# One order of wide and narrow products in the up projection, and twelve pairs of places for the weight parts of the first projections

## The chip, the core and the metric

The kernel runs on one core of one Trainium2 chip. The metric is the device time of one execution in microseconds. The time before is 1240.1 us, the median of three runs (1239.98 to 1240.11).

## What is computed

One layer of a hybrid decoder trunk, in float32, for 256 tokens of width 2048 with 16 learned tokens ahead of them (272 rows in all). Cut to what matters:

```python
h = concatenate([meta, x])                        # 272 x 2048
u = rms_norm(h, g_pre_mix)
z_pool, v_conv, g_conv, gate_a, gate_b = split(u @ w_in)   # 1024, 1024, 1024, 2048, 2048 columns
y_a = causal_multiscale_pool(z_pool, w_pool_grp, pool_scale) @ w_pool_out
y_b = conformer_conv(v_conv, g_conv, ...) @ w_conv_out
m = sigmoid(gate_a) * y_a + sigmoid(gate_b) * y_b
h = h + rms_norm(m @ w_o, g_post_mix)
u = rms_norm(h, g_pre_mlp)
f = square(relu(u @ w_up)) @ w_down               # 2048 -> 8192 -> 2048
h = h + rms_norm(f, g_post_mlp)
return h[16:]
```

## The kernel before

**Every product in three.** Each float32 operand is split into two parts in TensorE's reduced float32 format: the high part is a rounding copy by ScalarE, the low part the rest, a subtraction by VectorE. A product of two operands is then three matmuls: high by high, high by low, and low by high.

**The stream of weights.** All weights come as chunks of 128 x 2048 numbers (1 MB) in one fixed list, `stream` (lines 111 to 134). `open_chunk` (L161) takes the next chunk of the list, issues its DMA on SP's queue (L177) and makes two tiles for its parts; the cast (L180) writes the high part `hi`, the subtraction (L183) the low part `lo`. `fetch` (L200) keeps two chunks ahead. The parts live in three rooms each, `lo0` to `lo2` and `hi0` to `hi2`, which chunk n uses as n modulo 3, so a room is written again when the products of the chunk three places back have read it. Two chunks (`spare`, L128) get tiles of their own.

**Places.** A line is 16 numbers, 64 bytes, and four lines are 256 bytes. I call the position of an address within 256 bytes, counted in lines, its place: 0 to 3. `ROOMS` (L143) gives for each room the place where it starts and how many lines it has to spare; `part_tile` (L153) shifts the tile within its room so that the part starts at the wanted place. Before, every low part is at place 1; a high part is at place 2 where its chunk is in `standing_chunks` (the z columns of `w_in`, L117, and `w_up`, L130) and at place 1 elsewhere. The normed input `u` of the first projections lies at place 0, and the input `u2` of the up projection (in the tile `m`) at place 1. Rows of these tiles are whole multiples of 256 bytes, so each slice that a matmul reads has the place of its tile.

**First projections.** Three kinds of product come first: v (columns 1024 to 2047 of `w_in`), g (2048 to 3071) and z (0 to 1023), each in four products of 256 columns, in the order v0, g0, v1, g1, v2, g2, v3, g3, z0 to z3. Each product has two chunks of 8 x 128 rows and two accumulators. The weights are what stands in the array; the 272 columns of `u` stream through. For each of 16 blocks of rows and each accumulator `mm3` (L336) issues three matmuls: the high weights by the high `u`, the high weights by the low `u`, and the low weights by the high `u`: 96 a product. The first product, v0, is interleaved with the transposes that make `u`. While these products run, VectorE works off a queue of other items (`pending`), the taps of the causal convolution above all.

**The middle.** Gates, pool and convolution outputs and the mixing product `o` follow; in them and in the down projection the activations stand in the array and 512 columns of weights stream (`block_t`, L594).

**The MLP.** It runs in four passes over 2048 hidden columns each. A pass has four up products (`project` with `mm2`, L366 and L354) and then four down products (`project_t`). An up product has four weight chunks of 4 x 128 rows and four accumulators of 512 columns: the left 256 gather high by high and low by high, the right 256 gather high by low. `mm2_high` (L344) is one wide matmul over both halves of the accumulator (512 columns, the high and the low part of `u2` side by side); `mm2_low` (L349) is one narrow matmul over the left half (256 columns). For each chunk the kernel goes through the four accumulators, and for each through four blocks of rows, a wide and a narrow matmul for each block. In `mm2` the wide one goes first, but for the last of the 16 blocks: there the narrow one goes first and the wide one, which covers the whole accumulator, carries the flag that ends the accumulation. So each accumulator ends with two narrow and then two wide matmuls in a row, the second wide one being that which begins the next accumulator. When an accumulator is complete, `halves` copies the left half with ScalarE and adds the right one with VectorE; the squared relu and the split for the down projection follow.

The first up product of the first pass is written out by hand (lines 896 to 949), because `u2` is still being made: its first three chunks are worked off in halves of the tokens, all wide ones of a chunk and then all its narrow ones (`up_high`, `up_low`); its last chunk goes through `mm2`.

Of the kernel before, what the change touches and what calls it, by code (L numbers as in the profile page):

```python
# [9 lines left out]
F32R = mybir.dt.float32r  # L10
# [4 lines left out]
P = 128  # L15
CK = 4
CW = 512
# [5 lines left out]
def hybrid_block(ctx: ExitStack, tc: tile.TileContext, ins: dict, out: bass.AP):  # L23
# [7 lines left out]
    KD = D // P  # L31
    w_in = ins["w_in"][0]
# [9 lines left out]
    PW = NG * GD  # L42
# [9 lines left out]
    parts = ctx.enter_context(tc.tile_pool(name="parts", bufs=1))  # L52
# [4 lines left out]
    def f32(ap):  # L57
        return ap.bitcast(F32)

    def acc_tile(name):  # L60
        return psA.tile([P, CW], F32, tag="acc", name=name)
# [38 lines left out]
    def columns(w, k0, nk, c0, shape=(CK, CW)):  # L100

        ck, cw = shape
        return [(w[(k0 + kc) * P:(k0 + kc + ck) * P, c0:c0 + cw]
                 .rearrange("(k p) c -> p k c", p=P), shape) for kc in range(0, nk, ck)]
# [4 lines left out]
    HALF = (2 * CK, CW // 2)  # L109
    HALF_CW = CW // 2  # L110
    stream = []
    for h in range(CC // HALF_CW):
        for c0 in (PW, PW + CC):
            stream += columns(w_in, 0, KD, c0 + h * HALF_CW, HALF)
    standing_chunks = set()
    for h in range(PW // HALF_CW):
        standing_chunks.update(range(len(stream), len(stream) + KD // HALF[0]))  # L117
        stream += columns(w_in, 0, KD, h * HALF_CW, HALF)
    for n in range(2 * D // CW):
        stream += columns(w_in, 0, KD, G0 + n * CW)  # L120
    stream.append((w_grp.rearrange("g (k p) c -> p (g k) c", p=P), (NG * GD // P, GD)))
# [7 lines left out]
    for i in range(NP):  # L129
# [3 lines left out]
        for n in range(NB):  # L133
            stream += columns(w_down, i * KD, KD, n * CW)
    FIRST = KD // HALF[0]
# [1 line left out]
    at = {"n": 0}  # L137

    LINE = 16
    ROOMS = {"lo0": (1, 0), "lo1": (1, 0), "lo2": (1, 0), "hi0": (1, 1), "hi1": (2, 3),  # L143
             "hi2": (1, 1)}
    ready = {}

    def part_room(key, name):
        return parts.tile([P, CK * CW + ROOMS[key][1] * LINE], F32R, tag=key, name=name)

    for key in ROOMS:  # L150
        ready[key] = part_room(key, f"{key[:2]}_{key[2]}")

    def part_tile(tag, n, standing=False):  # L153
        key = f"{tag}{n % 3}"
        room = ready.pop(key) if key in ready else part_room(key, f"{tag}_{n}")
        start = ROOMS[key][0]
        to = 2 if standing else 1
        shift = (to - start) % 4 * LINE
        return room[:, shift:shift + CK * CW]

    def open_chunk():  # L161
        n = at["n"]
        at["n"] += 1
        src, (rows, width) = stream[n]
        raw = raws.tile([P, CK * CW], F32, tag="raw", name=f"raw_{n}")
        if n in spare:
            both = big.tile([P, 2, CK * CW], F32R, tag=spare[n], name=f"parts_{n}")
            hi, lo = both[:, 0, :], both[:, 1, :]
        else:
            hi, lo = part_tile("hi", n, n in standing_chunks), part_tile("lo", n)  # L170
        raw, hi, lo = (t.rearrange("p (k c) -> p k c", k=rows) for t in (raw, hi, lo))
        pieces = rows if n < FIRST + 1 else 1
        k = rows // pieces
        loads = 4 if n < FIRST else 1
        for i in range(loads):
            sl = slice(i * rows // loads, (i + 1) * rows // loads)
            nc.sync.dma_start(raw[:, sl, :], src[:, sl, :])  # L177

        def high(sl):
            nc.scalar.copy(hi[:, sl, :], raw[:, sl, :])  # L180

        def low(sl):
            nc.vector.tensor_sub(lo[:, sl, :], raw[:, sl, :], f32(hi[:, sl, :]))  # L183

        def piece(i):
            def f():
                sl = slice(i * k, (i + 1) * k)
                high(sl)
                low(sl)
            return f  # L190
        todo = [piece(i) for i in range(pieces)]
        if n in spare:
            todo = [lambda: high(slice(0, rows)), lambda: low(slice(0, rows))]
        opened.append((hi, lo, todo))
# [5 lines left out]
    def fetch(ahead=2):  # L200

        for c in range(ahead + 1):
            if c == len(opened) and at["n"] < len(stream):
                open_chunk()
            if c < len(opened):
                split_pieces(c)
        flush()
        return opened.pop(0)[:2]
# [51 lines left out]
    for b in range(2, XB):  # L260
        open_chunk()
        load_x(nc.sync, b)
# [81 lines left out]
    def mm2_high(acc, hi, act, k, cs, start, ts=slice(0, T), stop=False):  # L344
        off = act.shape[3] - T
        nc.tensor.matmul(acc.rearrange("p (a t) -> p a t", a=2)[:, :, ts], hi[:, k[0], cs],  # L346
                         act[:, k[1], :, off + ts.start:off + ts.stop], start=start, stop=stop)

    def mm2_low(acc, lo, act, k, cs):  # L349
        off = act.shape[3] - T  # L350
        nc.tensor.matmul(acc[:, :T], lo[:, k[0], cs], act[:, k[1], 0, off:],  # L351
                         start=False, stop=False)

    def mm2(acc, hi, lo, act, k, cs, first, last):  # L354


        if last:
            mm2_low(acc, lo, act, k, cs)
        mm2_high(acc, hi, act, k, cs, first, stop=last)
        if not last:  # L360
            mm2_low(acc, lo, act, k, cs)

    def acc_tiles(name, n=CW // P):
        return [acc_tile(f"acc_{name}_{j}") for j in range(n)]
# [1 line left out]
    def project(act, nk, evac, name, mm=mm2, width=CW, shape=HALF, fill=0.0):  # L366

        ck, cw = shape
        accs = [acc[:, :width] for acc in acc_tiles(name, cw // P)]
        for kc in range(nk // ck):  # L370
            hi, lo = fetch()
            for j, acc in enumerate(accs):
                for k in range(ck):
                    kk = kc * ck + k
                    mm(acc, hi, lo, act, (k, kk), slice(j * P, (j + 1) * P), kk == 0, kk == nk - 1)
                if kc == nk // ck - 1:
                    flush(1)
                    evac(j, acc)
                if fill:
                    drain(fill * P / cw)  # L380
# [52 lines left out]
    def pieces_to(n):  # L433

        while first["split"] < min(n, (FIRST + 1) * HALF[0]):
            c = first["split"] // HALF[0]
            if c == at["n"]:
                open_chunk()
            opened[c][2].pop(0)()
            first["split"] += 1  # L440
# [212 lines left out]
    hi, lo = fetch()  # L653
    for g in range(NG):
        for j in range(GK):
            q = g * GK + j
            acc = acc_tile(f"acc_grp_{q}")[:, :T]
# [242 lines left out]
    def up_high(kc, t):  # L900

        for k in range(CK):
            for j, acc in enumerate(accs):
                kk = kc * CK + k
                mm2_high(acc, ups[kc][0], u2, (k, kk), slice(j * P, (j + 1) * P),
                         t == 0 and kk == 0, slice(t * P, (t + 1) * P))

    def up_low(kc):
        for k in range(CK):
            for j, acc in enumerate(accs):  # L910
                mm2_low(acc, ups[kc][1], u2, (k, kc * CK + k), slice(j * P, (j + 1) * P))
# [28 lines left out]
    hi, lo = fetch()  # L940
# [3 lines left out]
    for j, acc in enumerate(accs):  # L944
        for k in range(CK):
            kk = 3 * CK + k
            mm2(acc, hi, lo, u2, (k, kk), slice(j * P, (j + 1) * P), False, kk == KD - 1)
        flush(1)
        evac_up(0)(j, acc)
# [65 lines left out]
    n = KD // CK - 3  # L1015
    for kc in range(n):
        hi, lo = fetch()
# [54 lines left out]
```

## Time and profile before

| | |
|---|---|
| Median of three runs | 1240.1 us |
| The profiled execution | 1240.15 us |
| Its span, first to last instruction of the program | 1238.2 us |
| Matmuls, and their share of the span in the profile | 6572, 99% |
| VectorE, ScalarE busy | 65%, 44% |
| Moved by DMA | 237.22 MB, mean 192 GB/s |

The profile is of one execution. Its page gives the busy time of each engine; the chain of work that ended last, followed back from the last instruction to what released each step; and groups of instructions by source line (L346 is line 346 of the kernel). A row of a group reads: line, engine, operation, what it writes and reads, count | busy us, mean ns of one | idle time of the engine ahead of them and what ended it. Matmuls are pipelined: each is shown longer than the step from its start to that of the next, so what a matmul costs is read from starts, not from its length.

### The profile page before, as it was taken

How to read it: one execution, taken by the hardware profiler on the slowest of the kernel's cores; microseconds unless marked ns; L12 is line 12 of the kernel's file. 1: busy time of each engine (PE TensorE's matmuls, PEld its weight loads, DVE VectorE, ACT ScalarE, POOL GpSimd, SP SyncE). 2: the span in 40 equal slices, each digit the busy share in tenths (PEclk: the TensorE clock that was granted, in tenths of full speed). 3: DMA queues.
4: the chain of work that ended last, by engine and by line, in shares of the span. 5: the costliest groups of instructions: out<-in, count | busy, mean ns of one | idle time of the engine just before them, and what ended most of it. 6: DMA issues, size and time to landing. Idle time of an engine off the chain costs nothing.

```text
span 1238.2 us, 15685 instructions
## 1 busy us (share of the span) xinstructions
PE 1227.5 (99%) x6572; PEld 1062.4 (86%) x6572; DVE 807.5 (65%) x938; ACT 542.2 (44%) x571; POOL 6.2 (0%) x18
## 2 busy tenths in 40 slices
PE   9999999999999999999999999999999999999997
PEld 8999988888888888898888888888888888888886
DVE  5799978999676654685744457544465545556555
ACT  6633344443573443555433344433344433435432
POOL 1000000000000000000000000000000000000000
PEclk9999999999999999999999999999999999999999
DMA  8655555555648565556565665655656655656551
GB/s 264 212 180 171 170 195 183 201 195 186 197 154 312 180 230 190 192 170 188 187 200 183 194 199 175 204 188 189 201 174 200 198 183 197 190 187 201 185 189 68
DMA packets 130757, 237.22 MB, mean 192 GB/s; under 512 B 3985, under 2 KB 29905, under 8 KB 130160
## 3 DMA queue, kind: packets, MB, share of 16 engines
q1 hardware_dynamic: 128768, 229.78, 57.0%
q0 software_dynamic: 768, 4.35, 0.9%
q10 hardware_dynamic: 1152, 2.11, 0.5%
q8 instruction: 51, 0.84, 0.3%
q14 instruction: 18, 0.15, 0.0%
HBM read 234.12 MB, written 2.10 MB: 191 GB/s over the span
## 4 chain that ended last, share of the span: by engine, by line
PE 98%; DVE 1%; DMA 0%; ACT 0%; DVEq 0%; issue 0%; ACTq 0%
PE acc_dn L599 26%; PE acc_up L346 19%; PE acc_gate L599 14%; PE acc_up L351 10%; PE acc_o L599 5%; PE acc_v L341 4%; PE acc_z L341 4%; PE acc_g L341 4%; PE acc_co L599 4%; PE acc_po L599 4%; PE acc_f_last L599 2%; PE acc_o_last L599 2%; DMA x_in<-in_x_dram 0%; PE xt L288 0%; PE ht L824 0%; PE mt L719 0%
## 5 line engine op out<-in xcount | busy, mean ns | idle before, releaser
L183 DVE TENSOR_TENSOR lo<-raw,hi 128x2048 fp32r<-128x2048 f32 (+1 forms) x236 | 495.1, 2101 | 357.7 <-ACT hi L180 357.2
L180 ACT CAST hi<-raw 128x2048 fp32r<-128x2048 f32 (+1 forms) x236 | 414.1, 1758 | 560.8 <-PE acc_dn L599 190.7
L346 PE MATMUL acc_up<-m,hi 128*128 128x512 f32 (+1 forms) x1008 | 339.0, 389 | 0.0
L599 PE MATMUL acc_dn<-hi,f_act 128*128 128x512 f32 x960 | 296.4, 389 | 0.0
L351 PE MATMUL acc_up<-m,lo 128*128 128x256 f32 x992 | 263.9, 279 | 0.0
L346 PEld LDWEIGHTS acc_up<-m,hi 128*128 128x128 f32 x1008 | 182.8, 188 | 35.8
L599 PEld LDWEIGHTS acc_dn<-hi,f_act 128*128 128x128 f32 x960 | 180.2, 188 | 37.6
L351 PEld LDWEIGHTS acc_up<-m,lo 128*128 128x128 f32 x992 | 185.7, 188 | 5.4
L599 PE MATMUL acc_dn<-lo,f_act 128*128 128x512 f32 x480 | 186.7, 389 | 0.0
L599 PE MATMUL acc_gate<-hi,u 128*128 128x512 f32 x512 | 158.6, 390 | 0.0
L409 DVE SCALAR_TENSOR_TENSOR c<-a,taps,c 128x256 f32<-128x256 f32 x240 | 115.5, 484 | 6.6
L599 PEld LDWEIGHTS acc_gate<-hi,u 128*128 128x128 f32 x512 | 96.1, 188 | 19.9
L599 PEld LDWEIGHTS acc_dn<-lo,f_act 128*128 128x128 f32 x480 | 90.1, 188 | 18.5
L599 PE MATMUL acc_gate<-lo,u 128*128 128x512 f32 x256 | 99.6, 389 | 0.0
L599 PE MATMUL acc_o<-hi,m 128*128 128x512 f32 x192 | 59.5, 390 | 0.0
L599 PEld LDWEIGHTS acc_gate<-lo,u 128*128 128x128 f32 x256 | 48.1, 188 | 10.0
L341 PE MATMUL acc_v<-u,hi 128*128 128x272 f32 x256 | 49.8, 293 | 0.0
L341 PE MATMUL acc_z<-u,hi 128*128 128x272 f32 x256 | 48.4, 288 | 0.0
L341 PE MATMUL acc_g<-u,hi 128*128 128x272 f32 x256 | 47.5, 286 | 0.0
L599 PEld LDWEIGHTS acc_o<-hi,m 128*128 128x128 f32 x192 | 36.0, 188 | 7.4
L599 PE MATMUL acc_co<-hi,s_act 128*128 128x512 f32 x128 | 40.3, 391 | 0.0
L341 PEld LDWEIGHTS acc_z<-u,hi 128*128 128x128 f32 x256 | 40.2, 189 | 0.0
(222 smaller groups left out, 1060.6 us busy)
## 6 DMA issues: line engine op xcount, KB each, us to landing
raw<-in_w_up_dram SPq DMA_DIRECT2D x64, 1024.0 KB, 5.4
raw<-in_w_down_dram SPq DMA_DIRECT2D x64, 1024.0 KB, 5.2
raw<-in_w_in_dram SPq DMA_DIRECT2D x54, 1024.0 KB, 5.1
raw<-in_w_o_dram SPq DMA_DIRECT2D x16, 1024.0 KB, 5.2
raw<-in_w_pool_out_dram SPq DMA_DIRECT2D x8, 1024.0 KB, 5.2
raw<-in_w_conv_out_dram SPq DMA_DIRECT2D x8, 1024.0 KB, 5.5
raw<-in_w_in_dram SPq DMA_DIRECT2D x8, 256.0 KB, 7.5
h<-in_x_dram POOLq DMA_DIRECT2D x1, 2048.0 KB, 11.0
```

Of the source, the lines that this page charges most:

```text
L180: nc.scalar.copy(hi[:, sl, :], raw[:, sl, :])
L183: nc.vector.tensor_sub(lo[:, sl, :], raw[:, sl, :], f32(hi[:, sl, :]))
L341: nc.tensor.matmul(acc, w[:, k[0], cs], act[:, k[1], a, off:], start=first and n == 0, stop=last and n == 2)
L346: nc.tensor.matmul(acc.rearrange("p (a t) -> p a t", a=2)[:, :, ts], hi[:, k[0], cs], act[:, k[1], :, off + ts.start:off + ts.stop], start ...
L351: nc.tensor.matmul(acc[:, :T], lo[:, k[0], cs], act[:, k[1], 0, off:], start=False, stop=False)
L409: nc.vector.scalar_tensor_tensor(c, conv["a"][:, q, i:i + T], taps[:, q, i:i + 1], c, op0=ALU.mult, op1=ALU.add)
L599: nc.tensor.matmul(acc, act(kk)[:, a_, ts_], w_[:, k, :], start=kk == 0 and n == 0, stop=kk == nk - 1 and n == 2)
```

## The change

Two things change, both in the order or the addresses of work that stays the same.

In `mm2` the last block no longer reverses its pair: every block has the wide matmul first and the narrow one second, and the narrow one of the last block carries the flag that ends the accumulation. The argument `skip_group_check` tells the program's checker, not the chip, that this flag covers half of the accumulator only.

The chunks of the twelve first products no longer have one pair of places. Product number i (0 to 11, in the order above) has its high parts at place i modulo 4 and its low parts at place i divided by 4: v0 (0, 0), g0 (1, 0), v1 (2, 0), g1 (3, 0), v2 (0, 1), g2 (1, 1), v3 (2, 1), g3 (3, 1), z0 (0, 2), z1 (1, 2), z2 (2, 2), z3 (3, 2). All other chunks keep their places: (2, 1) for `w_up`, (1, 1) elsewhere. So that any place can be had, each of the six rooms is now three lines longer than its 2048 numbers.

```diff
+    for h in range(PW // HALF_CW):
+        stream += columns(w_in, 0, KD, h * HALF_CW, HALF)
+    first_products = len(stream)
     standing_chunks = set()
-    for h in range(PW // HALF_CW):
-        standing_chunks.update(range(len(stream), len(stream) + KD // HALF[0]))
-        stream += columns(w_in, 0, KD, h * HALF_CW, HALF)
...
-    ROOMS = {"lo0": (1, 0), "lo1": (1, 0), "lo2": (1, 0), "hi0": (1, 1), "hi1": (2, 3),
-             "hi2": (1, 1)}
+    PLACES = {n: (2, 1) for n in standing_chunks}
+    PLACES.update({n: (n // FIRST % 4, n // FIRST // 4) for n in range(first_products)})
+    KEYS = [f"{tag}{b}" for tag in ("lo", "hi") for b in range(3)]
...
-        return parts.tile([P, CK * CW + ROOMS[key][1] * LINE], F32R, tag=key, name=name)
+        return parts.tile([P, CK * CW + 3 * LINE], F32R, tag=key, name=name)
...
-    def part_tile(tag, n, standing=False):
+    def part_tile(tag, n):
         key = f"{tag}{n % 3}"
         room = ready.pop(key) if key in ready else part_room(key, f"{tag}_{n}")
-        start = ROOMS[key][0]
-        to = 2 if standing else 1
-        shift = (to - start) % 4 * LINE
+        place = PLACES.get(n, (1, 1))[("hi", "lo").index(tag)]
+        shift = (place - 1 - 3 * KEYS.index(key)) % 4 * LINE
         return room[:, shift:shift + CK * CW]
...
     def mm2_high(acc, hi, act, k, cs, start, ts=slice(0, T), stop=False):
         off = act.shape[3] - T
         nc.tensor.matmul(acc.rearrange("p (a t) -> p a t", a=2)[:, :, ts], hi[:, k[0], cs],
-                         act[:, k[1], :, off + ts.start:off + ts.stop], start=start, stop=stop)
+                         act[:, k[1], :, off + ts.start:off + ts.stop], start=start, stop=stop,
+                         skip_group_check=True)
 
-    def mm2_low(acc, lo, act, k, cs):
+    def mm2_low(acc, lo, act, k, cs, stop=False):
         off = act.shape[3] - T
         nc.tensor.matmul(acc[:, :T], lo[:, k[0], cs], act[:, k[1], 0, off:],
-                         start=False, stop=False)
+                         start=False, stop=stop, skip_group_check=True)
 
     def mm2(acc, hi, lo, act, k, cs, first, last):
-        if last:
-            mm2_low(acc, lo, act, k, cs)
         mm2_high(acc, hi, act, k, cs, first, stop=last)
-        if not last:
-            mm2_low(acc, lo, act, k, cs)
+        mm2_low(acc, lo, act, k, cs, stop=last)
```

More of the change, by code (lines that the diff above doesn't have):

```diff
@@ L142, in hybrid_block @@
     LINE = 16
-    ROOMS = {"lo0": (1, 0), "lo1": (1, 0), "lo2": (1, 0), "hi0": (1, 1), "hi1": (2, 3),
-             "hi2": (1, 1)}
+    PLACES = {n: (2, 1) for n in standing_chunks}
+    PLACES.update({n: (n // FIRST % 4, n // FIRST // 4) for n in range(first_products)})
+    KEYS = [f"{tag}{b}" for tag in ("lo", "hi") for b in range(3)]
     ready = {}
     def part_room(key, name):
-        return parts.tile([P, CK * CW + ROOMS[key][1] * LINE], F32R, tag=key, name=name)
-    for key in ROOMS:
+        return parts.tile([P, CK * CW + 3 * LINE], F32R, tag=key, name=name)
+    for key in KEYS:
         ready[key] = part_room(key, f"{key[:2]}_{key[2]}")
-    def part_tile(tag, n, standing=False):
+    def part_tile(tag, n):
         key = f"{tag}{n % 3}"
         room = ready.pop(key) if key in ready else part_room(key, f"{tag}_{n}")
-        start = ROOMS[key][0]
-        to = 2 if standing else 1
-        shift = (to - start) % 4 * LINE
+        place = PLACES.get(n, (1, 1))[("hi", "lo").index(tag)]
+        shift = (place - 1 - 3 * KEYS.index(key)) % 4 * LINE
         return room[:, shift:shift + CK * CW]
@@ L169, in open_chunk @@
         else:
-            hi, lo = part_tile("hi", n, n in standing_chunks), part_tile("lo", n)
+            hi, lo = part_tile("hi", n), part_tile("lo", n)
         raw, hi, lo = (t.rearrange("p (k c) -> p k c", k=rows) for t in (raw, hi, lo))
```

## The prediction, made before the changed kernel ran

> **What bounds the kernel now.** I read the page first, then the chain of work that ended last in order of time, then TensorE's timeline and its busy time in chosen stretches. From the page:
>
> ```profile
> span 1238.2 us, 15685 instructions
> ## 1 busy us (share of the span) xinstructions
> PE 1227.5 (99%) x6572; PEld 1062.4 (86%) x6572; DVE 807.5 (65%) x938; ACT 542.2 (44%) x571; POOL 6.2 (0%) x18
> ...
> PE 98%; DVE 1%; DMA 0%; ACT 0%; DVEq 0%; issue 0%; ACTq 0%
> ...
> L183 DVE TENSOR_TENSOR lo<-raw,hi 128x2048 fp32r<-128x2048 f32 (+1 forms) x236 | 495.1, 2101 | 357.7 <-ACT hi L180 357.2
> L180 ACT CAST hi<-raw 128x2048 fp32r<-128x2048 f32 (+1 forms) x236 | 414.1, 1758 | 560.8 <-PE acc_dn L599 190.7
> ```
>
> TensorE carries 98% of the chain, so the time is the sum of the steps from the start of one matmul to the start of the next. The change adds and removes no matmul; it can only alter those steps. Busy time is no help (ends are modelled, neighbours overlap). The chain gives steps for whole stages: start, length, engine, matmuls.
>
> ```profile
> 28.34 11.84 PE acc_g L341 x96
> ...
> 113.19 48.36 PE acc_z L341 x384
> ...
> 529.17 1.83 PE acc_up L346 x16
> 531.00 1.92 PE acc_up L351 x16
> ...
> 614.39 87.06 PE acc_dn L599 x384
> ```
>
> A g product takes 11.84 / 96 = 123.3 ns a matmul, z 48.36 / 384 = 125.9 ns. Both have 272 columns, the same three matmuls in turn and the same stored u; what differs is the place of the high weight parts, 1 in g and 2 in z. So the place is worth 2.6 ns a matmul there: real, and small. Down products take 87.06 / 384 = 226.7 ns for 512 columns.
>
> The up projection doesn't run at one speed. Next is the busy time of the wide matmuls alone (L346) in stretches laid on the products: start:end, length, busy (count), clock, DMA share, GB/s. In each pass over 2048 hidden columns there are four up products. The first row is the last weight chunk of the first pass's first product; the next three are that pass's other products. Then the second pass follows, each of its products cut into its first three chunks and its last one, and the whole third pass.
>
> ```profile
> 541.78:547.38 5.60, 5.31 (x16) 1.00 0.90 298
> 547.38:569.28 21.90, 21.62 (x66) 1.00 0.63 206
> 569.28:591.84 22.56, 22.28 (x66) 1.00 0.61 187
> 591.84:614.23 22.39, 22.11 (x65) 1.00 0.57 188
> 701.29:717.62 16.33, 16.33 (x48) 1.00 0.62 194
> 717.62:723.19 5.57, 5.29 (x17) 1.00 0.60 193
> 723.19:740.15 16.96, 16.96 (x49) 1.00 0.59 187
> 740.15:745.75 5.60, 5.32 (x18) 1.00 0.58 187
> 745.75:762.55 16.80, 16.80 (x49) 1.00 0.60 188
> 762.55:768.15 5.60, 5.32 (x18) 1.00 0.61 185
> 768.15:784.48 16.33, 16.33 (x49) 1.00 0.57 193
> 784.48:790.05 5.57, 5.29 (x17) 1.00 0.57 191
> 877.11:965.86 88.75, 87.61 (x256) 1.00 0.60 190
> ```
>
> I call four wide and four narrow matmuls in turn (one chunk for one accumulator) a unit; three chunks are 12 units. The same 96 matmuls take 16.33, 16.96, 16.80 and 16.33 us: 1.361, 1.413, 1.400 and 1.361 us a unit, at one clock (1.00) and in a repeating pattern (the third pass's 88.75 is the second's 21.90 + 22.56 + 22.40 + 21.90 = 88.76). I read these as three steady beats of the array, entered at a product's start and then kept. The last chunk of every product takes 5.57 to 5.60 us whatever the beat before, although its work is that of four units, 5.44 at the fast beat. The timeline of TensorE (start, length) shows why:
>
> ```profile
> 717.63 0.39 PE L346 MATMUL acc_up<-m,hi 128*128 128x512 f32 x1
> 717.85 0.28 PE L351 MATMUL acc_up<-m,lo 128*128 128x256 f32 x1
> 717.97 0.39 PE L346 MATMUL acc_up<-m,hi 128*128 128x512 f32 x1
> ...
> 722.50 0.39 PE L346 MATMUL acc_up<-m,hi 128*128 128x512 f32 x1
> 722.73 0.40 PE L351 MATMUL acc_up<-m,lo 128*128 128x256 f32 x2
> 722.96 0.63 PE L346 MATMUL acc_up<-m,hi 128*128 128x512 f32 x2
> 723.42 0.28 PE L351 MATMUL acc_up<-m,lo 128*128 128x256 f32 x1
> 723.54 0.40 PE L346 MATMUL acc_up<-m,hi 128*128 128x512 f32 x1
> 723.78 0.28 PE L351 MATMUL acc_up<-m,lo 128*128 128x256 f32 x1
> ```
>
> At 717.63 a pair of the fast beat takes 0.34 us. At 722.73 stand two narrow matmuls together, then two wide ones: the reversed last pair of an accumulator. Behind it, from 723.42 to 723.78, a pair takes 0.36. The reversal knocks the array out of its beat at every accumulator of the last chunk, and the next product inherits the beat that the last knock leaves.
>
> **The change, part by part.** *One order of wide and narrow.* Sixty-four accumulators lose their reversal (sixteen products of four). Without the knock nothing in a product disturbs its beat: 12 units on end keep it over chunk and accumulator boundaries, and a product boundary is no more than those. Passes two to four are entered from the down products (614.39 + 87.06 = 701.45), whose steps this edit doesn't touch, and the first product behind them runs at 1.361. I therefore let all four products of these passes run at that beat: 64 units x 1.361 = 87.1 us in place of 88.75, saving 1.7 a pass, 5.1 in three.
>
> The first pass is entered from the products that its split start leaves, and its last chunk before the first reversal isn't separately shown; the four rows take 5.60 + 21.90 + 22.56 + 22.39 = 72.45 us for 52 units. At the fast beat they would be 70.8 (-1.7), at the middle one 72.8 (+0.35), at the slow one 73.5 (+1.0). I take the middle one: that chunk starts among steps near 120 ns (531.00: 1.92 / 16) and its 5.60 is that of four middle units. Sum for this edit: -4.75.
>
> What waits on it costs nothing. The evacuation waits for the accumulator's last matmul, as before, now a narrow one. The write of a low part must wait for that narrow matmul, one step (under 0.13 us) behind the last reader of the high part; but it also waits for the cast of its chunk (1758 ns, and VectorE's idle time ahead of L183 is all put down to that cast), which starts only once the high part is free. Without that cover it would be 0.12 us a chunk on VectorE, and behind it stand only the next low parts and evacuations. In the first pass the last wide matmul of the first accumulator comes ahead of a narrow one and so needs the last low part of u2 one step sooner: 0 to 0.12 us, once, taken as 0. Faster up products ask for a chunk every 5.44 us; the down stage takes its 16 chunks in 87.06, the same rate, with no wait in the chain, so loads and splits keep up.
>
> *Twelve pairs of places.* The eight v and g products had (high, low) parts at (1, 1) and the four z at (2, 1): 8 x 11.84 + 48.36 = 143.1 us, counting 96 steady matmuls each. Now each product has another pair: high parts at 0 to 3 with low ones at 0, then at 1, then at 2. Two of the twelve are those known, 11.84 and 12.09 us. The other ten are shown nowhere for 272 columns, so I bound them. A column is worth (226.7 - 120) / 256 = 0.417 ns, by the down row and 531.00. The fastest step near this size is the 256-column one at 529.17, 1.83 / 16 = 114.4 ns; with 16 columns more, 121.1. The slowest is the slow beat: 1413 / 4 = 353.3 a pair of 768 columns, 33.3 above 768 x 0.417 = 320, or 16.7 a matmul: 113.3 + 16.7 = 130.0. So ten products take 116.3 to 124.8 us, the edit -2.9 to +5.7. I take the mean of the two steps measured at this very size, 124.6: 119.6 + 11.84 + 12.09 = 143.5, +0.45. That z was slower than g speaks for a little loss.
>
> [...]
>
> *The larger rooms* of the parts (three lines each) move only VectorE's and ScalarE's scratch behind them: 0.
>
> Sum: -5.1 + 0.35 + 0.45 = -4.3 us. The profiled execution took 1240.15 (span 1238.2 and 1.95 around it), the median of the three is 1240.1: **1235.8**.
>
> **The rivals.** *All fast*: the first pass falls into the fast beat too and the new places come out near their good bound: -5.1 - 1.7 - 2.9 = -9.7, 1230.4. For it: the fast beat is the one that most products find. Against: g and z lie above that bound.
>
> *Bad places*: the beats as forecast, the ten pairs at 130 ns: -4.75 + 5.7 = +0.95, 1241.1. For: z's step back. Against: it asks for the worst step of another stage in all ten.
>
> *The beat isn't inherited* (the other side): a product boundary alone, not the reversal, drops the array into the slow beat. Then in each pass the first product runs at 1.361 and three at 1.413: 21.8 + 67.8 = 89.6 against 88.75, +0.85 three times, the first pass +1.0, places +0.45: +4.0, 1244.1. It decides as soon as the second product of a pass needs over 22.2 us (a quarter of 88.75). For: beats were seen to change nowhere but in last chunks, which are also ends of products. Against: the timeline has the slower steps before the product ends.
>
> *Nothing happens*: neither the order nor the places set the steps, but what else uses the memory then: 1240.15. For: DMA shares differ a little between the stretches (0.57 to 0.63). Against: beats repeat between passes to 0.01 us, and 16.33 occurs at shares of 0.62 and 0.57. [...]
>
> **How the numbers follow.** Forecast 0.62; all fast, wholly or half, 0.15; bad places 0.10; not inherited 0.07; nothing 0.06. About 0.2%, 2.5 us, is what a measurement of this kernel tells from no change. Faster by more: the forecast but for a little, and all fast: 0.77. Within: nothing, bad places and that little: 0.17. Slower: 0.06. The range goes from two thirds of the way to all fast, 1232.2, to no change, 1240.2.
>
> **What would show it.** Right: all products of passes two to four at 21.8 us, no pairs of like matmuls at their ends, a pass at 87.1; the first pass near 72.8; twelve different first products between 11.6 and 12.5. Wrong: a second product over 22.2 us, last chunks still at 5.6, a wait of TensorE for the low parts, or first products above 12.5.

## The result, and the profile after

The changed kernel takes 1237.82 us (median of 13 runs, 1235.0 to 1238.32) against 1240.11 (13 runs, 1239.87 to 1240.39). The ratio is 0.9979, 95% interval 0.9971 to 0.9988: 2.3 us less. That is a gain, but a little over half of the 4.3 us that were forecast, and just inside the 0.2% that the prediction drew as its bound. The profiled execution took 1238.2 us, its span fell from 1238.2 to 1236.3.

First the wide matmuls of the up projection (now line 344) in the stretches of its products: start:end, length, busy (count), clock, DMA share, GB/s. The rows are the last chunk of the first pass's first product and its three other products, the four products of the second pass, and the whole third and fourth pass.

```profile
543.86:549.51 5.65, 5.65 (x16) 1.00 0.92 305
549.51:572.13 22.62, 22.62 (x66) 1.00 0.60 199
572.13:594.74 22.61, 22.61 (x66) 1.00 0.61 186
594.74:617.35 22.61, 22.61 (x65) 1.00 0.57 186
704.42:726.19 21.77, 21.77 (x64) 1.00 0.62 194
726.19:747.95 21.76, 21.76 (x65) 1.00 0.62 194
747.95:769.71 21.76, 21.76 (x65) 1.00 0.62 194
769.71:791.47 21.76, 21.76 (x65) 1.00 0.59 194
878.54:965.59 87.05, 87.05 (x256) 1.00 0.61 194
1052.66:1139.71 87.05, 87.05 (x256) 1.00 0.61 194
```

Where the passes had products of 21.9, 22.6, 22.4 and 21.9 us, every product of passes two to four is now at 21.76, the fast beat from its first unit to its last: 88.75 - 87.05 = 1.70 us less a pass, 5.1 in three. The timeline shows the boundary between the first two products of the second pass, at 726.19, where the reversal used to stand:

```profile
725.51 0.39 PE L344 MATMUL acc_up<-m,hi 128*128 128x512 f32 x1
725.74 0.28 PE L350 MATMUL acc_up<-m,lo 128*128 128x256 f32 x1
725.85 0.39 PE L344 MATMUL acc_up<-m,hi 128*128 128x512 f32 x1
726.08 0.28 PE L350 MATMUL acc_up<-m,lo 128*128 128x256 f32 x1
726.19 0.39 PE L344 MATMUL acc_up<-m,hi 128*128 128x512 f32 x1
726.42 0.28 PE L350 MATMUL acc_up<-m,lo 128*128 128x256 f32 x1
726.53 0.39 PE L344 MATMUL acc_up<-m,hi 128*128 128x512 f32 x1
```

A pair still takes 0.34 us on both sides: the array passes into the next product without a step out of place. The first pass kept one beat too, but the slow one: 5.65 + 22.62 + 22.61 + 22.61 = 73.49 us in place of 72.45, 1.04 more.

The rest was given back in the first projections. In the chain of waits (start, length, engine, matmuls):

```profile
28.71 12.04 PE acc_g L339 x96
...
54.81 12.05 PE acc_g L339 x96
66.86 12.14 PE acc_v L339 x96
79.01 11.85 PE acc_g L339 x96
90.85 12.09 PE acc_v L339 x96
102.94 12.05 PE acc_g L339 x96
114.99 48.58 PE acc_z L339 x384
163.57 146.91 PE acc_gate L595 x648
```

Each product now shows the price of its pair of places. The one that kept (1, 1), g2 at 79.01, takes the old 11.85 us. The one at (2, 1), v3, takes 12.09, which is what z had taken at that pair before. The others that can be read here cost about as much: 12.04 to 12.14, and the four z 12.15 in the mean (48.58 / 4). The first product, v0, is interleaved with transposes and shows no such row; from its first matmuls to the first g product it took 19.29 us, against 19.31 before, so its pair shows no price there. From the first g product to the first gate it is 163.57 - 28.71 = 134.86 us, against 133.21 before (a row of before, from the same view: the gates began at 161.55), 1.65 more.

```profile
161.55 146.89 PE acc_gate L599 x648
```

So -5.1 + 1.04 + 1.65 = -2.4 us. The first g product began 0.37 us later in this execution (28.71 against 28.34), which isn't the change's: the transfer of the input `x_in` took 5.99 us against 5.60, and the first v matmuls began at 9.42 against 9.03. With it the span's -1.9 is explained to 0.1 us. No new wait came up: VectorE still waits for the casts alone ahead of the low parts (354.1 of 354.5 us; 357.2 of 357.7 before).

```profile
L181 DVE TENSOR_TENSOR lo<-raw,hi 128x2048 fp32r<-128x2048 f32 (+1 forms) x236 | 495.1, 2101 | 354.5 <-ACT hi L178 354.1
```

### The profile page after: what moved, and what is told of

Its sections match the earlier page's. It is cut to its first block, busy times and chain, and to the rows that moved or that the text cites. A ratio compares the mean times of both kernels' runs of the same rounds, so it can differ in the third digit from the quotient of the medians.

```text
span 1236.3 us, 15686 instructions
## 1 busy us (share of the span) xinstructions
PE 1224.7 (99%) x6572; PEld 1061.3 (86%) x6572; DVE 807.6 (65%) x938; ACT 541.9 (44%) x571; POOL 6.2 (0%) x18
## 4 chain that ended last, share of the span: by engine, by line
PE 98%; DVE 1%; DMA 0%; ACT 0%; DVEq 0%; issue 0%; ACTq 0%
PE acc_dn L595 26%; PE acc_up L344 19%; PE acc_gate L595 14%; PE acc_up L350 10%; PE acc_o L595 5%; PE acc_v L339 4%; PE acc_z L339 4%; PE acc_g L339 4%; PE acc_co L595 4%; PE acc_po L595 4%; PE acc_f_last L595 2%; PE acc_o_last L595 2%; DMA x_in<-in_x_dram 0%; PE xt L286 0%; PE ht L820 0%; PE mt L715 0%
## 5 line engine op out<-in xcount | busy, mean ns | idle before, releaser
L181 DVE TENSOR_TENSOR lo<-raw,hi 128x2048 fp32r<-128x2048 f32 (+1 forms) x236 | 495.1, 2101 | 354.5 <-ACT hi L178 354.1
L350 PE MATMUL acc_up<-m,lo 128*128 128x256 f32 x992 | 272.5, 277 | 0.0
L344 PEld LDWEIGHTS acc_up<-m,hi 128*128 128x128 f32 x1008 | 187.0, 188 | 39.5
```

## The experiments

The first three are edits of the changed kernel; a later one says which of them it builds on. Each is compared with the kernel before on the same chip; its medians there were 1240.2 us.

### The order alone

```diff
-    PLACES.update({n: (n // FIRST % 4, n // FIRST // 4) for n in range(first_products)})
+    PLACES.update({n: (2, 1) if n // FIRST >= 8 else (1, 1) for n in range(first_products)})
```

> The changed kernel with the places of before for the first products ((1, 1) for v and g, (2, 1) for z), so the order alone. Theory (the beat is inherited once nothing knocks the array out of it): passes two to four at 87.05 us each, 1.7 less than before; first products back at 143.1 us; the first pass (last chunk of its first product and its three other products) at the middle beat 72.8 us, or at 73.5 (slow) or 70.8 (fast). Time 1240.1 - 5.1 + 0.35 = 1235.4 (1236.0 slow, 1233.3 fast). Rival (the gain of the change came with the new places): 1240.1, and products of 21.9 to 22.6 us again.

Measured: 1235.93 us (1235.61 to 1236.23), ratio 0.9966 (0.9954 to 0.9979). The stretches of the wide matmuls are the first pass behind its split start, and the second pass:

```profile
541.57:615.06 73.49, 73.49 (x208) 1.00 0.63 199
702.12:789.18 87.06, 87.06 (x256) 1.00 0.62 194
```

The rival falls: the gain is there with the old places, and it is the predicted one, with the first pass at the slow beat also without the new places. The order alone is 1.9 us better than the change.

### The places alone

```diff
     def mm2(acc, hi, lo, act, k, cs, first, last):
+        if last:
+            mm2_low(acc, lo, act, k, cs)
         mm2_high(acc, hi, act, k, cs, first, stop=last)
-        mm2_low(acc, lo, act, k, cs, stop=last)
+        if not last:
+            mm2_low(acc, lo, act, k, cs)
```

> The changed kernel with the reversed last pair of before in each accumulator, so the places alone. Theory: first products 1.7 us longer, as in the changed kernel, and passes of 88.75 us with last chunks of 5.6 us: 1241.8. Rival (places cost nothing, the loss came from the first up pass): 1240.1. On the spread of the changed kernel's times (1235.0 to 1238.3): if it comes from first products that find no steady beat, this kernel spreads by over 1 us too and the order alone does not; if it comes from which beat the first up pass finds, it is the other way round.

Measured: 1241.84 us (11 runs, 1241.71 to 1242.44), ratio 1.0014 (1.0005 to 1.0023): a loss of 1.6 us, as expected. On the spread neither statement held as written: this kernel and the order alone both keep within 0.8 us. The stretches hold something else: three products of the first pass, then the second pass.

```profile
549.34:571.74 22.40, 22.11 (x65) 1.00 0.62 202
571.74:593.64 21.90, 21.62 (x66) 1.00 0.61 191
593.64:616.19 22.55, 22.27 (x65) 1.00 0.57 187
703.25:792.01 88.76, 87.62 (x256) 1.00 0.61 190
```

In the kernel before, the same three products went fast, slow, middle (21.90, 22.56, 22.39); here they go middle, fast, slow. The order of the cycle is the same and only its start moved. Four knocks to a product that move the array one step of slow, middle, fast, slow each make just one step in all, since four is three and one. That gave the theory for the later runs. It also means that the three products take 66.85 us in both kernels, whichever beat they begin with; without the knocks, the beat of the entry decides (22.62, 22.61 and 22.61 us in the change).

### The order, and all first products at (1, 1)

```diff
-    PLACES.update({n: (n // FIRST % 4, n // FIRST // 4) for n in range(first_products)})
+    PLACES.update({n: (1, 1) for n in range(first_products)})
```

> The new order, and all twelve first products at places (1, 1). Theory (a product's steps are set by its places): z falls from 12.09 to 11.84 us a product, 1.0 us less than with the order alone: 1234.4 with a first pass at the middle beat, 1235.1 slow, 1232.4 fast. Rival (z is slower for another reason than its places, such as what VectorE does then): z stays at 12.09 and the time is that of the order alone.

Measured: 1234.55 us (1234.26 to 1235.19), ratio 0.9955 (0.9943 to 0.9968). The chain of waits of the order alone has the first row for z, that of this kernel the second:

```profile
112.97 48.36 PE acc_z L339 x384
```

```profile
113.24 47.36 PE acc_z L339 x384
```

One place of the high parts is worth 1.00 us over 384 matmuls, 2.6 ns each, and the rival falls. The profiled run took 1235.19, with its first pass at 73.49, the slow beat; the other four runs took 1234.26 to 1234.62, about the time expected of the middle one. So the first pass seems to find different beats in different runs of one kernel; only the profiled run shows its beat.

### One knock left in

An edit of the kernel before this one, in the hand-written last chunk of the first pass's first product:

```diff
-            mm2(acc, hi, lo, u2, (k, kk), slice(j * P, (j + 1) * P), False, kk == KD - 1)
+            cs = slice(j * P, (j + 1) * P)
+            if j == 0 and kk == KD - 1:
+                mm2_low(acc, lo, u2, (k, kk), cs)
+                mm2_high(acc, hi, u2, (k, kk), cs, False, stop=True)
+            else:
+                mm2(acc, hi, lo, u2, (k, kk), cs, False, kk == KD - 1)
```

> As the one before, but the very first accumulator of the first pass's last hand-written chunk keeps its reversed last pair: one knock in place of 64. Theory (a knock sets the beat anew, and behind that one the trace of before showed pairs of 226 + 114 ns): the first pass runs at the fast beat, 5.5 + 65.3 = 70.8 us, time 1232.4. Rival (a knock always leaves a slow beat, or the beat of a product does not hang on what ran before it): the first pass stays where it is without the knock, 72.8 to 73.5 us, time 1234.4 to 1235.1.

Measured: 1232.43 us (1232.39 to 1234.23), ratio 0.9938 (0.9924 to 0.9951). Four runs lie within 0.04 us of 1232.4, the time of the fast beat. The profiled one is the fifth, 1234.23, and its first pass is at the middle beat:

```profile
540.56:613.36 72.80, 72.72 (x208) 1.00 0.63 201
```

With a knock moving the array one step, these are entries at the middle beat (then fast) and at the slow one (then middle). The expectation held in the times of four runs, but no profile shows the fast case yet, and the entry isn't the same in all runs. The next kernels are made to mend both.

### A steady entry, with none, one and two knocks

Ahead of the first pass's last chunk stand the narrow matmuls of a chunk whose parts are at place 0. In the chain of the kernel before, they are the second of these rows; the first is the narrow matmuls of the chunk ahead of it, with parts at place 1:

```profile
535.27 1.92 PE acc_up L351 x16
...
540.06 1.89 PE acc_up L351 x16
```

The chunk at place 1 steps by 1.92 / 16 = 120 ns, the one at place 0 by 118 in the mean. The next three kernels, with all first products at (1, 1), have that chunk at place 1 as well, and none, one or two reversed pairs.

```diff
-            both = big.tile([P, 2, CK * CW], F32R, tag=spare[n], name=f"parts_{n}")
-            hi, lo = both[:, 0, :], both[:, 1, :]
+            skip = LINE if spare[n] == "s1" else 0
+            both = big.tile([P, skip + 2 * CK * CW], F32R, tag=spare[n], name=f"parts_{n}")
+            hi, lo = both[:, skip:skip + CK * CW], both[:, skip + CK * CW:]
...
-            if j == 0 and kk == KD - 1:
+            if j in (0, 1) and kk == KD - 1:
```

> The order of the change, all first products at (1, 1), and the parts of the third up chunk (one of the two with tiles of their own) one line further, at place 1 in place of 0, so that the narrow matmuls just ahead of the first pass's last chunk step by an even 120 ns, where at place 0 they drift between 117 and 119. Theory (the first pass's beat hangs on the phase in which that drift leaves the array): the entry becomes the same in every run, the spread falls below 0.5 us, and the time is one of 1232.4 (fast), 1234.4 (middle) or 1235.1 (slow). Rival (the beat is drawn anew in each run for another reason): times keep falling into two groups.

> As the one before, with one reversed pair, at the first accumulator of the first pass's last chunk. Theory (a knock moves the array one step round the cycle slow, middle, fast, slow): from 1235.1 to 1234.4, from 1234.4 to 1232.4, or from 1232.4 to 1235.1, whichever the one before has. Rival (a knock draws a beat at random): no such relation between the two, and a spread of 2 us.

> As the one before, with a second reversed pair, at the second accumulator. Theory (cycle of three): the three kernels with none, one and two knocks have the three times 1232.4, 1234.4 and 1235.1 in cyclic order, so exactly one of them is at 1232.4, the fast beat in all four passes. Rival: none is, or two agree.

Measured: none 1234.49 us (1234.33 to 1234.79), one 1232.55, two 1235.28; ratios 0.9954 (0.9942 to 0.9966), 0.9945 (0.9933 to 0.9956) and 0.9967 (0.9955 to 0.9978). The first pass in the three profiles, in that order:

```profile
540.66:613.46 72.80, 72.80 (x208) 1.00 0.64 201
```

```profile
540.91:611.68 70.77, 70.70 (x208) 1.00 0.64 206
```

```profile
540.68:614.12 73.44, 73.30 (x208) 1.00 0.62 199
```

The same 416 matmuls take the middle, the fast and the slow time, as one reversed pair after the other is added: the cycle of three, in its order, at the three expected times. In the profile of the second kernel one sees a knock do it:

```profile
541.49 0.28 PE L351 MATMUL acc_up<-m,lo 128*128 128x256 f32 x1
541.61 0.39 PE L345 MATMUL acc_up<-m,hi 128*128 128x512 f32 x1
541.84 0.40 PE L351 MATMUL acc_up<-m,lo 128*128 128x256 f32 x2
542.08 0.63 PE L345 MATMUL acc_up<-m,hi 128*128 128x512 f32 x2
542.55 0.28 PE L351 MATMUL acc_up<-m,lo 128*128 128x256 f32 x1
542.66 0.39 PE L345 MATMUL acc_up<-m,hi 128*128 128x512 f32 x1
542.89 0.28 PE L351 MATMUL acc_up<-m,lo 128*128 128x256 f32 x1
```

From the narrow matmul at 541.49 to that at 541.84 it is 0.35 us, from 542.55 to 542.89 it is 0.34. The runs of the three kernels keep within 0.5, 0.4 and 0.8 us, but for one run of the second and one of the third, so the entry seems steady. Those two lie 5.1 and 3.8 us above the medians (1237.6 and 1239.07). Neither was profiled, but the record has their mean granted clock: 0.993 and 0.995, where the other runs of these kernels have 0.997 to 0.999. Estimated from these, 0.3 to 0.5% of 1235 us is 4 to 6 us, so a lower clock accounts for their size, and no other beat is needed. What lowered it isn't shown.

### One knock in the second pass

The new order with all first products at (1, 1), and in `project`:

```diff
-                    mm(acc, hi, lo, act, (k, kk), slice(j * P, (j + 1) * P), kk == 0, kk == nk - 1)
+                    cs = slice(j * P, (j + 1) * P)
+                    if name == "up10" and j == 3 and kk == nk - 1:
+                        mm2_low(acc, lo, act, (k, kk), cs)
+                        mm2_high(acc, hi, act, (k, kk), cs, False, stop=True)
+                    else:
+                        mm(acc, hi, lo, act, (k, kk), cs, kk == 0, kk == nk - 1)
```

> The order of the change, all first products at (1, 1), and a single reversed pair at the end of the second pass's first product. Theory (one knock at the fast beat leaves the slow one, which is inherited until the down products reset it): that product 21.77 us, the three behind it 22.61 each, the pass 2.55 us longer (89.6), passes three and four 87.05; 1234.4 + 2.55 = 1237.0 with a first pass at the middle beat, 1237.7 at the slow one. Rival (each product finds its beat by itself, the reversal costs only its own four matmuls): 0.01 us longer, 1234.4 to 1235.1.

Measured: 1237.76 us (10 runs; nine from 1236.91 to 1237.87, and one at 1242.89, again at a lower mean granted clock, 0.994 against 0.997 to 0.999), ratio 0.9983 (0.9975 to 0.9992). The four products of the second pass, and the third pass:

```profile
701.23:723.01 21.78, 21.71 (x65) 1.00 0.62 194
723.01:745.62 22.61, 22.61 (x65) 1.00 0.61 188
745.62:768.24 22.62, 22.62 (x66) 1.00 0.60 185
768.24:790.85 22.61, 22.61 (x65) 1.00 0.56 187
877.92:964.98 87.06, 87.06 (x256) 1.00 0.62 194
```

Two matmuls changed places and the pass is 2.56 us longer, nearly all of it in the three products behind, which are untouched. The beat is inherited, and the down products reset it: the next pass is back at 87.06.

### Other places for the up projection

The kernel with a steady entry and one knock, and:

```diff
+    per_pass = len(standing_chunks) // NP
+    for i, n in enumerate(sorted(standing_chunks)):
+        PLACES[n] = ((2, 1), (1, 1), (2, 0), (3, 1))[i // per_pass]
```

> As the kernel with one knock, but the four up passes have the (high, low) weight parts at places (2, 1), (1, 1), (2, 0) and (3, 1). Theory (which beats there are hangs on the places, and (2, 1) against a stream at place 1 is what makes 1.360 us a unit): the passes two to four run at other beats than 1.360, (1, 1) at about 4 x (227 + 120) = 1388 ns a unit, 88.8 us a pass, from the 227 ns of down matmuls and the 120 ns of narrow ones where both operands are at place 1. Rival (the beats come from the alternation alone): all four passes at 87.05.

Measured: 1242.29 us, one run. The passes two to four, at (1, 1), (2, 0) and (3, 1):

```profile
698.68:789.12 90.44, 90.44 (x256) 1.00 0.59 187
876.18:966.61 90.43, 90.43 (x256) 1.00 0.59 187
1053.68:1143.78 90.10, 90.10 (x256) 1.00 0.60 187
```

All three are 3.0 to 3.4 us longer than 87.06, so the rival falls. The passes at (1, 1) and (2, 0) take 22.61 us a product (90.44 / 4), which is also the slow beat's time at (2, 1), so the time alone can't tell them from it. The starts in the trace can: at (1, 1) the wide matmuls step about 232, 240 and 236 ns in turn; at (2, 0) they step 233 or 234, with the narrow ones at 120 but for the first few; in the slow beat at (2, 1), in the first pass of the change, they step 232 to 235, with narrow ones of 117 to 122. So the theory holds in kind, with one pass of one run for each pair: which beats there are hangs on the places. My number for (1, 1), 88.8, was too low by 1.6 us: steps of one stage didn't carry over to another even at equal places.

### The best version again

> The kernel with one knock a second time, since one of its six runs was 5 us above the others. Theory (the entry of the first pass is the same in every run): runs within 0.5 us of 1232.5. Rival (the first pass, or a later one, finds another beat in some runs): single runs again 2 to 5 us higher.

Measured: 1232.63 us (1232.34 to 1232.97, 5 runs), ratio 0.9938 (0.9925 to 0.9952). No run stood out this time, and none had a clock below 0.997. This kernel (new order, all first products at (1, 1), a steady entry, one reversed pair) beats the one before by 7.6 us and the change by about 5.

## Why the prediction came out as it did

The sign was right, and the size a little over half. The time lies within the 0.2% of no change, to which the prediction had given a chance of 0.17, against 0.77 for a larger gain. Two terms of the sum were too small, by 0.69 and 1.20 us, and both erred the same way, so nothing cancelled.

**The mechanism was right.** Beats that a product enters with and keeps, the reversal as what breaks them, and the gain in passes two to four were all read from the trace of before; 1.7 us a pass was predicted and 1.70 measured in the change, and the second pass took 87.05 or 87.06 us in the seven profiles read of kernels that kept the order and the places (2, 1) there. The single knock in the second pass shows cause and inheritance directly (2.56 us). That the beats follow each other in a fixed order was not foreseen.

**The first pass was mis-sized.** The step was "I take the middle one", +0.35 us; the changed kernel's profile has the slow one, +1.04. One reason given (the last chunk's 5.60 us is that of four middle units) was no evidence: in the kernel before, that chunk held three knocks with units behind them and so ran through several beats. The conclusion was true of that one execution: by the starts in its trace it entered the chunk with steps of 231, 117, 234 and 118 ns, the middle beat. But the entry isn't fixed. With the places alone the chunk was entered at 233, 121, 233 and 117, the slow beat, and the program with all first products at (1, 1) took the slow beat in its profiled run and, by its times, the middle one in others. The change's lowest run, 1235.0, lies 2.8 us below its median, about the 73.49 - 70.77 = 2.7 that separate slow from fast; its clock, 0.997, was that of the others, but it wasn't profiled. What draws the beat at the entry is open.

**The places were mis-sized.** The step was "the mean of the two steps measured at this very size", +0.45 us; measured was +1.65. The new pairs that could be read took 12.04 to 12.15 us a product, all near the worse of the two known (12.09), and (1, 1) was the best. The sign was right and the bounds held; the mean treated the one good pair as one of two equal cases.

**The hidden costs were nothing, as said**: TensorE sat idle 0.0 us ahead of the matmuls of the up and down projections in the change's profile, so it waited neither for low parts nor for loads, at 194 GB/s in the second pass against 190 before.

**The rivals.** *All fast* falls in the profiled execution, with the slow beat in the first pass and no product that can be read below 11.85 us. *Not inherited* falls with the second to fourth products at 21.76 us. *Nothing happens* falls with the order alone (1235.93 us, 4.3 less than before): in this stream a place is worth 1.00 us in z and the beat 2.7 us in the first pass. Of *bad places* under a third came true (1.65 of 5.7 us). The time ended between the forecast and that rival, inside the range.

## What to carry to other kernels

In a dense stream of matmuls on float32 data, look at the steps from start to start, product by product: the same work may take different steady times at one clock, as the up products of the change did here (22.61 us in the first pass, 21.76 in the others, all at 1.00). Here one pair out of order in the second pass cost 2.56 us, nearly all of it in the three products behind it, up to the end of the stage. Keep the order regular over product boundaries, choose the places of the weight parts by measurement for each stage (at (1, 1) in place of (2, 1) z took 1.00 us less and an up pass 3.4 us more), and make the entry into a stage the same in every run. A product that is sized by analogy with another stage is a guess.

## What the runs showed of the hardware that I had not expected

Three beats were seen in the up projection with places (2, 1): the same instructions at the same clock (1.00) take 1.360, 1.400 or 1.413 us a unit, and repeat that over 416 matmuls and more. One exchanged pair moves the array to the next of the three in a fixed order (72.80, 70.77, 73.44 us with none, one and two knocks). The first product behind the down products was at the fast beat wherever it was read with places (2, 1): 16.33 us for its first 12 units in the kernel before, 21.77 in the change and 21.78 with the knock in the second pass, and whole second passes of 87.06 us in six other kernels. With other places the steady steps were others, and the passes took 90.44, 90.43 and 90.10 us. Why there are three, and what makes them, was not measured.
